# One z unit moved out of the first stage, tile-by-tile pool waits, and block sums between the z units of a DeltaNet encoder layer

## The chip, the cores and the metric

The kernel runs on one NeuronCore of a Trainium2 chip. The core has a matrix engine (TensorE, written PE in the profile, with its weight loads as PEld), a vector engine (VectorE, DVE), a scalar engine (ScalarE, ACT), a small general engine (GpSimd, POOL) and an engine that mostly issues transfers (SyncE, SP). Each engine runs its own instructions in order; they wait for each other through semaphores. SBUF is the on-chip memory, PSUM holds the results of matrix products in eight banks, and transfers between the chip's main memory and SBUF are DMAs. The metric is device time in microseconds; lower is better.

## The reference

The layer works on 1024 tokens plus 16 learned ones, with 1024 features, all in float32. What matters here is the combined input projection and where its columns go:

```python
h = rmsnorm(h_res, norm1_w[l])
proj = h @ w_in[l]
(q, k, v, z, b_raw, a_raw, sc_b, sc_c, sc_x, gate_a, gate_b) = jnp.split(proj, SPLIT_POINTS, axis=-1)
o_dn = gated_deltanet_bidir(q, k, v, z, ...)     # ends with o * silu(z), 8 heads of 128 columns
y_a = o_dn @ w_branch_dn[l]
y_b = (sc_b * conv3(sc_c * sc_x)) @ w_branch_sc[l]
merged = sigmoid(gate_a) * y_a + sigmoid(gate_b) * y_b
h_res = h_res + merged @ w_out[l]
h2 = rmsnorm(h_res, norm2_w[l]); gu = h2 @ w_gate_up[l]
h_res = h_res + (silu(gu[..., :D_FF]) * gu[..., D_FF:]) @ w_down[l]
out = rmsnorm(h_res, final_norm_w)
```

So z is needed for each of 8 heads, and gate_a and gate_b are two 1024-column products that share the moving operand h.

## The kernel before, in words

**Float32 by parts.** Every operand is split into a high part (a rounded copy, made by ACT in `split`, line 101) and a low part (the rest, made by DVE, line 102). A product of 128 features is then three matmuls: high by high, high by low, low by high. A z unit, which is the z of one head for all 1024 tokens, is two halves of 512 tokens; a half is `dense` (lines 134 to 136): 8 blocks of features by 3, so 24 matmuls of 128x128 by 128x512 into one PSUM bank. A unit is 48 such matmuls.

**The first stage** (pools `c1`, `d1`, `dn`; closed by `ph1.close()`) runs the projections of q, k and v, the short convolution, some gates and some z units as PE work, and beside it the scans of the eight heads, each a long chain of small operations on all engines. A planner written into the kernel (the times in `T`, the lanes, `run_streams`, `pump`) decides while the kernel is built how the two are interleaved; the order of all engines is then fixed by `manual_schedule`. Units are taken from `fill_units`, whose last entries are the z units of heads 0 to `ZH`-1 (`u_z`, line 341 for the matmuls, 474 and 478 for the tanh and the product on ACT and DVE, 480 for the transfer to `z_d`). `ZH` is 5. The last steps of the last head are the scaling of its rows (line 936, DVE), their transposes on PE (line 98), the copies to `vS` (951, ACT) and the transfer to `o_d` (953).

**The section behind it.** A new pool, `tp`, takes the SBUF range of the three closed pools. It is opened with the default waits: its first use waits until everything that used the closed pools is over, transfers too. Weights of the z units come through pools that stay open (`wload`, with two buffers `wh`/`wl` in turn; raw data through two raw buffers, and two more of `tp`). The section has the z units of heads 5, 6 and 7 (`z_rows`: line 1502 is the tanh on ACT, 1504 the product on DVE, 1505 the transfer), then the remaining gates.

**The remaining gates** go by pairs: gate_a and gate_b of 128 columns together, five pairs (`GH`=3 pairs were done in the first stage). They use a Strassen scheme of seven half-size products instead of eight. It needs sums of blocks on both sides. On the moving side `moving_sums` makes T1, T2, T3 and T4 from the blocks of h once, in steps of a few large DVE operations (lines 179 and 1409, 128x2048 elements each) and ACT casts (line 1457). On the weight side, each pair splits the raw gate weights (`first`), then `second` splits one block and forms the sums of blocks S1 to S4 (`sums`, lines 1416 and 179) and splits those (`stationary2`). The seven products of a pair (`product`, line 1440, 12 matmuls each) are, in the order of the code: A11·B11, A12·B21, S2·T2, S1·T1, S3·T3, S4·B22, A22·T4. S2·T2, S3·T3 and A22·T4 go on in the bank of A11·B11; S4·B22 goes on in the bank of S1·T1. Between two products in one bank the bank is read: line 1543 copies A11·B11 (ACT), 1555 copies behind S2·T2 (ACT), 1557 copies behind S1·T1 (ACT), and line 1409 adds from a bank on DVE, followed by a tanh (line 1508) on ACT.

**What sets the order.** From the opening of `tp` to the end of pair 0 (`border0`), DVE, PE and ACT issue their instructions of that region in the order of the code (`manual_schedule` for these three engines). Later work, which has no fixed order, may still be put between them: the framework's scheduler, which plans with its own model of times, takes an instruction of later code where it believes an engine to be free and the inputs to be ready. SP is free in this sense too. Behind `border0` all order is the scheduler's.

**PSUM banks** come in three groups: `pm` (2 banks, `psm`), `pe` (3 banks, `psd`), `pd` (3 banks, `pss`). `psz` takes from the first two in turn, `psany` from all three. The z units use `psany`.

## Time and profile before

| | |
|---|---|
| median of 3 runs | 2007.11 us (2007.06 to 2009.29) |
| profiled execution | 2003.46 us, of which its span 2001.7 us |
| mean granted TensorE clock | 0.996 |
| PE busy | 1974.2 us (99%) |
| PE weight loads busy | 1720.7 us (86%) |
| DVE busy | 1398.8 us (70%) |
| ACT busy | 837.2 us (42%) |

Times in the profile count from the first instruction of the span. The matmuls of 512 columns start 0.227 us apart when nothing holds them up, while each is listed with 0.39 us because they are pipelined; so a busy PE is not always at its rate, and gaps are best read from starts. A row of the timeline gives start, duration, engine, line, operation, output and inputs by the program's names, shapes, and the number of merged instructions; what stands in square brackets is the idle time of the engine before it and what ended it. "issue" stands where nothing in the profile ended the wait. In the windows, each row is a stretch of time with the busy time of each engine, the number of its instructions, the granted clock, and the DMA load.

### The profile page before, as it was taken

How to read it: one execution, taken by the hardware profiler on the slowest of the kernel's cores; microseconds unless marked ns; L12 is line 12 of the kernel's file. 1: busy time of each engine (PE TensorE's matmuls, PEld its weight loads, DVE VectorE, ACT ScalarE, POOL GpSimd, SP SyncE). 2: the span in 40 equal slices, each digit the busy share in tenths (PEclk: the TensorE clock that was granted, in tenths of full speed). 3: DMA queues.
4: the chain of work that ended last, by engine and by line, in shares of the span. 5: the costliest groups of instructions: out<-in, count | busy, mean ns of one | idle time of the engine just before them, and what ended most of it. 6: DMA issues, size and time to landing. Idle time of an engine off the chain costs nothing.

```text
span 2001.7 us, 31862 instructions
## 1 busy us (share of the span) xinstructions
PE 1974.2 (99%) x11999; PEld 1720.7 (86%) x11999; DVE 1398.8 (70%) x3020; ACT 837.2 (42%) x1964; POOL 108.0 (5%) x407
## 2 busy tenths in 40 slices
PE   9999999999999999999899999999999999999998
PEld 8999999999999999888688888887888888888887
DVE  6888688888888888844945544469866666656575
ACT  6472354636464646343344221224323333334344
POOL 2011101010101010100000000000000000000000
PEclk9999999999999999999999999999999999999999
DMA  3122221212222212222236743123666345477654
GB/s 133 65 90 74 59 86 59 75 59 75 59 75 59 86 59 65 75 85 91 94 112 239 248 151 112 63 85 107 240 231 216 140 150 188 157 276 244 193 170 172
DMA packets 124689, 251.00 MB, mean 125 GB/s; under 512 B 44981, under 2 KB 46438, under 8 KB 122103
## 3 DMA queue, kind: packets, MB, share of 16 engines
q1 hardware_dynamic: 123959, 247.92, 37.2%
q8 instruction: 94, 1.54, 0.3%
q10 hardware_dynamic: 576, 1.05, 0.1%
q14 instruction: 60, 0.49, 0.1%
HBM read 180.67 MB, written 68.25 MB: 124 GB/s over the span
## 4 chain that ended last, share of the span: by engine, by line
PE 47%; DVE 3%; ACT 1%; issue 1%; DMA 1%; SPq 0%; DVEq 0%; ACTq 0%
PE pd L1440 13%; PE pe L1440 6%; PE pm L1440 4%; PE pe L1894 1%; PE pe L1895 1%; PE pe L1896 1%; PE pd L1894 1%; PE pd L1895 1%; PE pd L1896 1%; PE pd L135 1%; PE pd L134 1%; PE pe L135 1%; PE pe L134 1%; PE pd L136 1%; PE pe L136 1%; PE pm L1895 1%
## 5 line engine op out<-in xcount | busy, mean ns | idle before, releaser
L341 PE MATMUL pm<-hTh,wh 128*128 128x320 f32 (+4 forms) x1264 | 434.2, 349 | 0.4 <-ACT hTh L1103 0.2
L341 PE MATMUL pm<-al,wh 128*128 128x320 f32 (+4 forms) x1264 | 433.6, 348 | 0.0
L341 PE MATMUL pm<-hTh,wl 128*128 128x320 f32 (+4 forms) x1264 | 431.7, 347 | 0.0
L341 PEld LDWEIGHTS pm<-hTh,wh 128*128 128x128 f32 x1264 | 236.7, 188 | 12.6 <-issue 1.3
L341 PEld LDWEIGHTS pm<-hTh,wl 128*128 128x128 f32 x1264 | 237.0, 188 | 10.9 <-issue 0.4
L341 PEld LDWEIGHTS pm<-al,wh 128*128 128x128 f32 x1264 | 236.9, 188 | 10.3
L102 DVE TENSOR_TENSOR al<-raw,ring_h 128x1024 fp32r<-128x1024 f32 x73 | 88.6, 1223 | 64.8 <-ACT ring_h L101 64.4
L101 ACT CAST ring_h<-raw 128x1024 fp32r<-128x1024 f32 x73 | 76.8, 1053 | 107.1 <-PE pe L1896 35.5
L363 DVE SCALAR_TENSOR_TENSOR kq<-ra,wc,kq 128x520 f32<-128x520 f32 x128 | 96.6, 755 | 4.9 <-ACT kq L393 4.0
L990 DVE TENSOR_TENSOR wl<-raw,wh 128x512 fp32r<-128x512 f32 x114 | 77.4, 689 | 31.1 <-ACT wh L993 30.6
L889 ACT ACTIVATE w<-pd,small 128x128 f32<-128x128 f32 x128 | 39.8, 363 | 125.0 <-PE pd L882 124.3
L101 ACT CAST wh<-raw 128x1024 fp32r<-128x1024 f32 x48 | 50.4, 1050 | 77.7 <-PE pd L135 18.7
L500 DVE TENSOR_TENSOR fP<-fP,tm 128x135 f32<-128x135 f32 (+23 forms) x248 | 71.7, 289 | 5.1
L496 DVE TENSOR_TENSOR tm<-fP,fN 128x135 f32<-128x135 f32 (+23 forms) x248 | 71.5, 288 | 4.4
L993 ACT CAST wh<-raw 128x512 fp32r<-128x512 f32 x114 | 67.4, 621 | 3.7 <-issue 3.6
L102 DVE TENSOR_TENSOR wl<-raw,wh 128x1024 fp32r<-128x1024 f32 x48 | 58.5, 1220 | 13.6 <-ACT wh L101 13.4
L1409 DVE TENSOR_TENSOR b<-pd,b 128x512 f32<-128x512 f32 x22 | 15.2, 690 | 66.2 <-PE pd L1440 66.2
L1831 ACT ACTIVATE b<-b 128x512 f32<-128x512 f32 x22 | 13.9, 632 | 113.3 <-DVE b L1409 113.3
L1440 PE MATMUL pd<-b_hl,wh 128*128 128x512 f32 x176 | 54.4, 390 | 0.0
L856 ACT ACTIVATE jk<-NP 128x128 f32<-128x128 f32 x64 | 19.9, 311 | 78.8 <-DVE NP L852 77.7
L1440 PE MATMUL pd<-b,mB 128*128 128x512 f32 x204 | 50.7, 398 | 1.1 <-ACT s L1543 1.1
L876 DVE SCALAR_TENSOR_TENSOR r<-pd,negEG,vS 128x128 f32<-128x128 f32 x120 | 36.7, 345 | 20.9 <-PE pd L866 20.5
(590 smaller groups left out, 4724.6 us busy)
## 6 DMA issues: line engine op xcount, KB each, us to landing
raw<-in_w_in_dram SPq DMA_DIRECT2D x72, 512.0 KB
raw<-in_w_gate_up_dram SPq DMA_DIRECT2D x44, 512.0 KB
sums<-in_w_down_dram SPq DMA_DIRECT2D x22, 512.0 KB
t_d<-sums SPq DMA_DIRECT2D x11, 1024.0 KB
raw<-s_d SPq DMA_DIRECT2D x44, 256.0 KB
raw<-t_d SPq DMA_DIRECT2D x44, 256.0 KB
act_d<-b SPq DMA_DIRECT2D x43, 256.0 KB
raw<-act_d SPq DMA_DIRECT2D x33, 256.0 KB
```

What stands on the lines that cost most here:

```text
L101: nc.scalar.copy(hi, src)
L102: nc.vector.tensor_tensor(out=lo, in0=src, in1=hi.bitcast(F32), op=ALU.subtract)
L134: mm(po[:m, :n], wh[:, k, :m], xhk[:, t0:t0 + n], start=(k == 0), stop=False)
L135: mm(po[:m, :n], wh[:, k, :m], xlk[:, t0:t0 + n], start=False, stop=False)
L341: mm(po[:, :n], ww[:, k], f(k)[:, t0:t0 + n], start=i == 0, stop=i == 3 * KT - 1)
L363: nc.vector.scalar_tensor_tensor(out=acc, in0=raw[:, h0 + t:h0 + t + hn], scalar=wc[:, t, col:col + 1], in1=acc, op0=ALU.mult, op1=ALU.add)
L496: nc.vector.tensor_tensor(out=tv, in0=fP[:, 0:r, j:j + 1].broadcast_to([P, r, n]), in1=fN[:, j:j + 1, j + 1:32].broadcast_to([P, r, n]), o ...
L500: nc.vector.tensor_tensor(out=fP[:, 0:r, j + 1:32], in0=fP[:, 0:r, j + 1:32], in1=tv, op=ALU.subtract)
L990: nc.vector.tensor_tensor(out=u[1][1][:, k], in0=u[2][:, k], in1=u[1][0][:, k].bitcast(F32), op=ALU.subtract)
L993: nc.scalar.copy(u[1][0][:, k], u[2][:, k])
L1440: mm(po, x[:, k], y, start=k + i == 0 and not add_to, stop=k == 3 and i == 2, skip_group_check=add_to)
L1895: mm(bank[t], h_[:, c], l_[:, hi], start=False, stop=False)
```

## The change

`ZH` goes from 5 to 4: the first stage has four z units, the section behind it four (`z0` to `z3`, heads 4 to 7). Their banks come from `psz` in place of `psany`, so `pd` is left to the pairs. The pool `tp` is opened with `reuse_waits="tile"`: each of its tiles waits for what used its own addresses, and not for everything in the closed pools. `second` is cut in two: `block_sums` (split of one block, sums of blocks) and `second` (the splits of those). The order in the section is written anew: the steps of `moving_sums`, the weights of pair 0 and its block sums stand between the halves of the four z units, and no step is left behind the last z unit. `pair` becomes a generator; between the first two products of pair 0 and the rest of it stand the gate split and the block sums of pair 1. Pairs 0 and 1 are both inside `border0`. In a pair that isn't the last, S4·B22 now stands ahead of S3·T3. The last pair is as before.

```diff
-ZH = 5
+ZH = 4
...
-    tp = ctx.enter_context(tc.tile_pool(name="tp", bufs=1))
+    tp = ctx.enter_context(tc.tile_pool(name="tp", bufs=1, reuse_waits="tile"))
...
-            po = psany()
+            po = psz()
             dense(po, z_units[h - ZH], hx, C0 + META + sl.start, 512)
...
         def second():
+            stationary2(n, ru, rg, ru, A_)
+
+        def block_sums():
             split(*u_hl[n % 2], ru[:, 4:8])
             A_["A22"] = u_hl[n % 2]
             sums(rg, ru, rg[:, 0:4], rg[:, 4:8], ru[:, 0:4], ru[:, 4:8])
-            stationary2(n, ru, rg, ru, A_)
-        return A_, first, second
+        return A_, first, block_sums, second
...
+        else:
+            if n > 1:
+                first()
+                block_sums()
+            product(bank, A_["A11"], "B11")
+            nc.scalar.copy(o1[:, left], bank)
+            po = psz()
+            product(po, A_["A12"], "B21")
+            add(o1[:, left], po, o1[:, left])
+            half_turn(o1[:, left])
+            yield
+            if n:
+                second()
+            bank2 = psz()
+            product(bank, A_["S2"], "T2", True)
+            nc.scalar.copy(o1[:, right], bank)
+            product(bank2, A_["S1"], "T1")
+            nc.scalar.copy(o2[:, right], bank2)
+            yield
+            product(bank2, A_["S4"], "B22", True)
+            add(o1[:, right], bank2, o1[:, right])
+            half_turn(o1[:, right])
+            product(bank, A_["S3"], "T3", True)
+            add(o2[:, right], bank, o2[:, right])
+            half_turn(o2[:, right])
+            yield
+            product(bank, A_["A22"], "T4", True)
+            nc.scalar.activation(o2[:, left], bank, AF.Tanh, scale=0.5)
...
-    z0, z1, z2 = (z_rows(h) for h in range(ZH, H))
+    z0, z1, z2, z3 = (z_rows(h) for h in range(ZH, H))
     z_units.append(wload(w_in, unit(OZ + (ZH + 1) * P)))
     next(z0)
     next(sums_of_blocks)
     next(sums_of_blocks)
     next(z0)
-    z_units.append(wload(w_in, unit(OZ + (H - 1) * P)))
+    z_units.append(wload(w_in, unit(OZ + (ZH + 2) * P)))
     next(sums_of_blocks)
     next(z0)
     next(z1)
-    pair0 = pair_weights(0, GH)
     next(z1)
-    pair0[1]()
+    z_units.append(wload(w_in, unit(OZ + (ZH + 3) * P)))
+    next(sums_of_blocks)
     next(z1)
-    pair0[2]()
     next(z2)
+    weights0 = pair_weights(0, GH)
+    next(z2)
+    weights0[1]()
     next(sums_of_blocks)
     next(z2)
+    next(z3)
+    weights0[2]()
+    weights0[3]()
     next(sums_of_blocks)
+    next(z3)
     next(sums_of_blocks)
-    next(z2)
-    next(sums_of_blocks)
-    for n, j in enumerate(range(GH, KT)):
-        o1 = pair(n, j, *(pair_weights(n, j) if n else pair0))
-        if n == 0:
-            border0.close()
+    next(z3)
+    pair0 = pair(0, GH, *weights0)
+    weights1 = pair_weights(1, GH + 1)
+    next(pair0)
+    weights1[1]()
+    weights1[2]()
+    for _ in pair0:
+        pass
+    pair1 = pair(1, GH + 1, *weights1)
+    for _ in pair1:
+        pass
+    border0.close()
+    for n, j in enumerate(range(GH + 2, KT), 2):
+        for _ in pair(n, j, *pair_weights(n, j)):
+            pass
```

More of the change, by code (lines that the diff above doesn't have):

```diff
@@ L1415, in sums @@
         g0, g1, u0, u1 = rg[:, 0:4], rg[:, 4:8], ru[:, 0:4], ru[:, 4:8]
-        nc.vector.tensor_tensor(out=s1, in0=u0, in1=u1, op=ALU.add)
-        sub(s3, g0, u0)
-        sub(s2, s1, g0)
-        sub(s4_, g1, s2)
+        tt = nc.vector.tensor_tensor
+        tt(out=s1, in0=u0, in1=u1, op=ALU.add)
+        tt(out=s3, in0=g0, in1=u0, op=ALU.subtract)
+        tt(out=s2, in0=s1, in1=g0, op=ALU.subtract)
+        tt(out=s4_, in0=g1, in1=s2, op=ALU.subtract)
     def stationary2(j, ru, sa, sb, A_):
@@ L1530, in second, with pair @@
             sums(rg, ru, rg[:, 0:4], rg[:, 4:8], ru[:, 0:4], ru[:, 4:8])
-            stationary2(n, ru, rg, ru, A_)
-        return A_, first, second
-    def pair(n, j, A_, first, second):
+        return A_, first, block_sums, second
+    def pair(n, j, A_, first, block_sums, second):
         last = j == KT - 1
-        o1, o2 = s4(), s4()
+        o1, o2 = outs[n] = s4(), s4()
         bank = pss()
-        if not last:
-            if n:
-                first()
-            product(bank, A_["A11"], "B11")
-            nc.scalar.copy(o1[:, left], bank)
-            po = psz()
-            product(po, A_["A12"], "B21")
-            add(o1[:, left], po, o1[:, left])
-            half_turn(o1[:, left])
         if last:
             first()
-        if n:
+            block_sums()
             second()
-        bank2 = psz()
-        if not last:
-            product(bank, A_["S2"], "T2", True)
-            nc.scalar.copy(o1[:, right], bank)
-            product(bank2, A_["S1"], "T1")
-            nc.scalar.copy(o2[:, right], bank2)
-            product(bank, A_["S3"], "T3", True)
-            add(o2[:, right], bank, o2[:, right])
-            half_turn(o2[:, right])
-            product(bank2, A_["S4"], "B22", True)
-            add(o1[:, right], bank2, o1[:, right])
-            half_turn(o1[:, right])
-            product(bank, A_["A22"], "T4", True)
-            nc.scalar.activation(o2[:, left], bank, AF.Tanh, scale=0.5)
-        else:
+            bank2 = psz()
             product(bank, A_["S2"], "T2")
@@ L1586, in pair @@
             half_turn(o1[:, right])
+        else:
+            if n > 1:
+                first()
+                block_sums()
+            product(bank, A_["A11"], "B11")
[7 more added lines that the diff above has]
+                second()
+            bank2 = psz()
+            product(bank, A_["S2"], "T2", True)
[12 more added lines that the diff above has]
+            nc.scalar.activation(o2[:, left], bank, AF.Tanh, scale=0.5)
         nc.sync.dma_start(ta_d[j], o1)
         nc.sync.dma_start(tb_d[j], o2)
-        return o1
+        yield
+    outs = {}
     sums_of_blocks = moving_sums()
-    z0, z1, z2 = (z_rows(h) for h in range(ZH, H))
+    z0, z1, z2, z3 = (z_rows(h) for h in range(ZH, H))
     z_units.append(wload(w_in, unit(OZ + (ZH + 1) * P)))
@@ L1601, in encoder_layer @@
     next(z1)
-    pair0 = pair_weights(0, GH)
     next(z1)
-    pair0[1]()
+    z_units.append(wload(w_in, unit(OZ + (ZH + 3) * P)))
+    next(sums_of_blocks)
     next(z1)
-    pair0[2]()
     next(z2)
+    weights0 = pair_weights(0, GH)
+    next(z2)
+    weights0[1]()
     next(sums_of_blocks)
     next(z2)
+    next(z3)
+    weights0[2]()
+    weights0[3]()
     next(sums_of_blocks)
+    next(z3)
     next(sums_of_blocks)
-    next(z2)
-    next(sums_of_blocks)
-    for n, j in enumerate(range(GH, KT)):
-        o1 = pair(n, j, *(pair_weights(n, j) if n else pair0))
-        if n == 0:
-            border0.close()
+    next(z3)
[13 more added lines that the diff above has]
+            pass
+    o1 = outs[KT - 1 - GH][0]
     warm2 = keep.tile([P, 1], F32, name="warm2")
```

## The prediction

> **What bounds the kernel now.** I read the page's head first, then stretches of 10 us around the border behind the first stage, then PE's timeline there, then the chain of waits in that window.

> ```profile
> span 2001.7 us, 31862 instructions
> PE 1974.2 (99%) x11999; PEld 1720.7 (86%) x11999; DVE 1398.8 (70%) x3020; ACT 837.2 (42%) x1964; POOL 108.0 (5%) x407
> ```

> PE is the bound: no edit here removes a matmul, so a gain can only be time in which PE stands or runs slowly. In the stretches (PE, PEld, DVE, ACT, POOL busy; clock; DMA) I look for that:

> ```profile
> 970.00:980.00 10.00, 10.00 (x46) 8.26 (x45) 9.32 (x13) 1.70 (x3) 0.00 (x0) 1.00 0.42 160
> 980.00:990.00 10.00, 5.50 (x25) 4.22 (x23) 9.53 (x7) 3.86 (x5) 0.00 (x0) 0.98 0.33 105
> 990.00:1000.00 10.00, 6.07 (x14) 4.10 (x14) 10.00 (x9) 4.40 (x4) 0.00 (x0) 0.67 0.07 27
> 1000.00:1010.00 10.00, 9.56 (x36) 7.80 (x37) 6.01 (x6) 4.57 (x7) 0.00 (x0) 0.84 0.35 115
> ```

> From 980 to 1000 PE is busy for little more than half, DVE for nearly all, and the clock sinks to 0.67. PE's timeline:

> ```profile
> 945.96 0.39 PE L134 MATMUL pm<-hTh,wh 128*128 128x512 f32 x1
> ...
> 967.50 0.39 PE L136 MATMUL pe<-hTh,wl 128*128 128x512 f32 x1
> ...
> 979.90 0.39 PE L1440 MATMUL pd<-hTh,wh 128*128 128x512 f32 x1
> ...
> 985.12 0.39 PE L1440 MATMUL pm<-hTh,wl 128*128 128x512 f32 x1
> 991.38 0.77 PE L1440 MATMUL pd<-hTh,wh 128*128 128x512 f32 x1 [5.88 <-DVE s L1504]
> ...
> 996.21 0.50 PE L1440 MATMUL pd<-hTh,wl 128*128 128x512 f32 x1
> 998.56 0.50 PE L1440 MATMUL pd<-hTh,wh 128*128 128x512 f32 x1 [1.85 <-DVE s L1504]
> 998.90 0.40 PE L1440 MATMUL pd<-al,wh 128*128 128x512 f32 x1
> 1000.43 4.33 PE L1440 MATMUL pd<-b,mB 128*128 128x512 f32 x12 [1.14 <-ACT s L1543]
> 1004.60 2.90 PE L1440 MATMUL pe<-b,mB 128*128 128x512 f32 x12
> ```

> From 945.96 two z units (96 matmuls) take until 967.50 plus one slot: 21.54 over 95 intervals, 0.2267 us each, PE's rate. The third unit's 48 would then end at 978.61; the next product starts at 979.90, so 1.29 are lost. From 979.90 to 1004.60 there are 24+12+2+12 = 50 matmuls, 11.34 at the rate, in 24.70: 13.36 lost. Together **14.65 us lost**, the whole budget of this change. The 14 matmuls at 991.38 to 998.90 are A11·B11 of pairs 1 and 2, which the scheduler put into the gap; S2·T2 of pair 0 starts at 1000.43. The chain that leads there:

> ```profile
> 948.85 4.16 issue
> 953.10 2.29 DVE mA L179
> ...
> 995.55 2.37 DVE mA L1409 x2
> 998.00 1.90 ACT b L1457
> 999.90 0.49 ACT s L1543
> 1000.43 4.33 PE pd L1440 x12
> ```

> So DVE, from the first sum of blocks (953.10) through the T4 sum, then ACT's cast of T4 and, queued behind it, the copy of A11·B11 that S2·T2 needs. And DVE starts 4 us late:

> ```profile
> L480 SPq DMA_DIRECT2D z_d<-rb x5: 319/320/327, 925.0 to 948.9; - x5
>   DVE mA L179: 4.3, 1
> ```

> (tile `rb`, the second row under "who waited for it"): the pool waited for the first stage's last transfer, issued at 948.9 and over about 4.2 later. `mA` itself lies elsewhere.

> **The change, part by part.**

> *The moved unit.* 48 matmuls, 48 x 0.2267 = 10.88 us, leave the first stage, so the section's first z matmul moves from 945.96 to about 935.1. The total stays. What might be uncovered is the last head's end:

> ```profile
> 933.07 0.28 DVE L936 TENSOR_SCALAR NP<-NP,small 128x128 f32<-128x128 f32 x1
> 934.40 0.60 PE L98 MATMUL pd<-ident,NP 128*128 128x128 f32 x4
> ```

> DVE is through with the last head at 933.35, before the unit that goes begins on PE, so I charge 0. The unit's two products on DVE, its splits and its one or two z transfers go with it; SP is nearly idle there.

> *Pool waits.* The first user of `tp` no longer waits for the z transfer. DVE's last work of the first stage then ends at about 936.5 to 937, and T1 can follow at once; with the old waits it would start at 937.1 + 4.2 = 941.3.

> *The new order.* I walk it with DVE at 2.21 us for a 2048-element operation back to back (2.29 alone), 2.28 for the pair of 1024, 1.14 for a weight's low part, 0.60 for 512, and 1.90, 1.00 and 0.55 for ACT's casts of 2048, 1024 and 512, 0.1 for a hand-over. PE does eight halves of 5.44 from 935.1. The weights of the fourth z unit wait for the buffer that the second unit frees, at 935.1 + 21.8 = 956.9: tanh, cast, and DVE has its low part at 958.8. So DVE, which has come through T1, T2 and the low parts by 955.8, waits 3.0; a start up to 3 us later than 936.5 costs nothing. Then 1.14 + T3 6.70 + 0.60 to 967.2; 2.05 for ACT (high T3, tanh); 0.60; 0.95 for the cast of the gate weights, whose buffer the third unit frees; 1.14, T4's first step 2.21, low T3 2.21, 0.60 to 977.0; one split and four sums 3.0; casts and low parts of S 3.4 (one hand-over of 1.1 in it) to 983.5; T4's second step to 985.7. ACT then casts T4 (1.90), does the last z half's tanh (0.55) and the copy (0.55): **S2·T2 starts at 988.9** in place of 1000.43. PE has been through the z units and two products at 984.0, so it stands for **4.9 us**; nothing can fill this, because pair 1 is now fixed behind pair 0, and pair 2's raw weights come into buffers that pair 0 frees at 983. With the old pool waits the walk gives 990.8, so tile waits are worth 1.9 here (between 0 and 2.3).

> *Clock after that gap.* After the 6.0 us gap of before, eleven intervals from 991.38 to 996.21 took 0.439 each, 2.5 lost over twelve; the twelve from 1000.43 took 4.17 for 2.72, 1.45 lost. I take 2.0, the middle; ends 0 and 3.95. [...]

> *Order inside a pair.* S4·B22 right behind S1·T1 must wait for the copy from their bank, A22·T4 right behind S3·T3 for the add:

> ```profile
> 1007.54 0.59 ACT L1557 COPY s<-pe 128x512 f32<-128x512 f32 x1 [1.21 <-PE pe L1440]
> 1010.32 0.69 DVE L1409 TENSOR_TENSOR s<-pd,s 128x512 f32<-128x512 f32 x1 [2.73 <-PE pd L1440]
> 1011.05 0.63 ACT L1508 ACTIVATE s<-s 128x512 f32<-128x512 f32 x1 [2.43 <-DVE s L1409]
> ```

> S1·T1 from 1004.60 leaves its slot at 1007.32 and the copy ends at 1008.13: 0.85. The next product would follow S3·T3 at 1010.06 and the add ends at 1011.01: 1.0. Pair 1's splits of S now stand behind its half turn on ACT: from A12·B21's slot, 0.26 to the add, 0.69, 0.63, cast 1.05, low part 1.22: 3.9. Pairs 0 and 1 have 0.85 + 1.0 each, pair 1 3.9 besides: **7.6 us of new waits** on PE. In pairs 2 and 3 the order is free, and I cost the swap at nothing: S3's own matmuls cover it. How the scheduler covers such a place shows in the last pair, whose S3 stands in the bank of S2:

> ```profile
> 1072.17 1.07 PE L1440 MATMUL pm<-b,mB 128*128 128x512 f32 x4
> 1073.08 3.00 PE L1440 MATMUL pd<-b,mB 128*128 128x512 f32 x12
> 1075.91 1.98 PE L1440 MATMUL pm<-b,mB 128*128 128x512 f32 x8
> ```

> Four matmuls (0.91) of another bank go ahead, and nothing stands. For pairs 0 and 1, pair 2 can give its first 24 matmuls (5.44): freed buffers at 983 plus a load of 3.8,

> ```profile
> 969.31 0.33 SPq L1521 DMA_DIRECT2D raw<-in_w_in_dram  x1
> 973.11 0.62 ACT L101 CAST u_hl<-raw 128x512 fp32r<-128x512 f32 x1 [2.64 <-DMA raw<-in_w_in_dram]
> ```

> plus cast and low part, so by about 991, ahead of the first wait at 994; its S2 and the rest can follow. All 7.6 could be covered, or none; I take 6.1 covered, since the last pair's was whole but the scheduler's times aren't the chip's: **1.5 left**. `psz` for the z units costs nothing: each bank is read at least 6 us before its next use in the walk.

> *Sum.* Lost before 14.65; after 4.9 + 2.0 + 1.5 = 8.4; gain 6.2. On the profiled execution (2003.46) that gives 1997.2; it stood 3.65 under the median of 2007.11 (spread 2.2), on which I forecast **2000.9**.

> **The rivals.** *Uncovered waits (ends slower).* In pairs 0 and 1 PE's queue has nothing from pair 2 where it waits, because the scheduler's model sees no gap or believes pair 2's weights late. Then 7.6 stand in full, and pair 1's 3.9 may drop the clock once more (2.5): 4.9 + 2.0 + 7.6 + 2.5 = 17.0, 2.3 more than before: 2009.5, and 2011.5 if the first drop costs 3.95. It decides once more than about 5 of the 7.6 stay and the clock falls again. For it: pair 1 can't be moved ahead any more, as it was at 991.38; against it: the last pair.

> *The first stage's end lies bare (slower too).* If the scans' last steps move with the planner's books, PE waits at 935 to 945 for up to the removed 10.88: 8.4 + 10.9 = 19.3, so 2011.8; past 6.2 of waiting the gain is gone. Against it: 933.35.

> *Tile waits change nothing.* If the pool waits as a whole all the same, S2 starts at 990.8: 2002.8.

> *DVE no longer late at all.* If the steps between (3.0, 2.05, 0.95, 1.1 of waiting) shrink so that S2 follows A12 at once, only 1.5 is left: 14.65 - 1.5 = 13.1 gained, 1994. Against it: buffers of z weights come free at PE's pace.

> **How the numbers follow.** Forecast 0.42; uncovered waits 0.25; bare end 0.10; pool as before 0.13; DVE in time 0.10. A measurement here can tell about 0.2% (4 us) from no change. The forecast lies beyond that with 0.38 of its 0.42 (its own range: 1997.3, nothing left of 2.0 and 1.5, to 2005), pool as before with 0.05 of 0.13, DVE in time wholly: faster 0.53. Uncovered waits are within it with 0.14, beyond with 0.11; the bare end 0.03 and 0.07: slower 0.18, same 0.29. The range 1995.5 to 2011 leaves out most of "DVE in time" and the worst of the slower two.

> **What would show it.** Right: the section's first z matmul at about 935 with no gap before it; T1's first operation within 2 us of the first stage's last DVE work and no row of "issue" of 4 us ahead of it; PE without a gap through eight halves; one gap of 4 to 6 us ahead of S2·T2, ended by the ACT copy (it stands in `pair`); small pieces of pair 2's A11·B11 between pair 0's and 1's products. Wrong: gaps of about 0.9 and 1.0 in both pairs and 3.9 in pair 1, a second stretch with a clock under 0.9, a wait for the transposes near 935, or T1 starting 4 us after a z transfer.

## The result, and the profile after

The changed kernel takes 2000.73 us (median of 6 runs, 1999.46 to 2003.42); the kernel before took 2008.8 us beside it (median of 6, 2007.06 to 2009.36). The ratio is 0.9965, with a 95% interval of 0.9953 to 0.9977: 7 us faster, between 4.6 and 9.4 (the two medians as they stand are 8.1 apart). The forecast was 2000.9 us.

The head of the page, the stretches around the border (columns as in the prediction) and PE's timeline of the changed kernel; its profiled execution took 2001.06 us:

```profile
span 1999.3 us, 31850 instructions
PE 1973.1 (99%) x11999; PEld 1719.5 (86%) x11999; DVE 1398.9 (70%) x3019; ACT 837.1 (42%) x1963; POOL 106.5 (5%) x407
```

```profile
980.00:990.00 10.00, 5.54 (x25) 4.26 (x23) 7.34 (x9) 4.52 (x5) 0.00 (x0) 1.00 0.33 113
990.00:1000.00 10.00, 8.92 (x32) 6.98 (x33) 8.26 (x10) 4.46 (x7) 0.00 (x0) 0.83 0.13 52
1000.00:1010.00 10.00, 9.16 (x41) 7.27 (x40) 3.27 (x6) 2.38 (x4) 0.00 (x0) 1.00 0.17 68
```

```profile
936.40 0.40 PE L134 MATMUL pe<-hTh,wh 128*128 128x512 f32 x1
...
985.15 0.39 PE L1441 MATMUL pe<-hTh,wl 128*128 128x512 f32 x1
990.41 4.40 PE L1441 MATMUL pd<-b,mB 128*128 128x512 f32 x12 [4.87 <-ACT s L1572]
994.64 2.90 PE L1441 MATMUL pm<-b,mB 128*128 128x512 f32 x12
998.22 0.50 PE L1441 MATMUL pm<-hTh,mB 128*128 128x512 f32 x1 [0.68 <-ACT s L1584]
1001.08 2.88 PE L1441 MATMUL pd<-b,mB 128*128 128x512 f32 x12
1004.80 3.01 PE L1441 MATMUL pd<-b,w 128*128 128x512 f32 x12 [0.84 <-DVE s L1409]
```

Before, three gaps (5.88, 1.85 and 1.14 us) lay ahead of S2·T2, with a clock of 0.67 from 990 to 1000; now there is one gap ahead of it, and the clock is 0.83 for one stretch. S2·T2 starts at 990.41 in place of 1000.43. What ends the gap is still the copy of A11·B11 (now line 1572), at the end of this piece of the chain of waits:

```profile
985.13 2.28 DVE mA L1409 x2
987.49 0.07 ACT b L1458
987.56 1.73 issue
989.29 0.59 ACT s L1503
989.88 0.48 ACT s L1572
990.41 4.40 PE pd L1441 x12
```

"issue" at 987.56 is the rest of ACT's cast of T4 (the row before it), behind which the last z tanh and the copy are queued.

One measure serves all kernels below: **the border's loss**, the distance from the section's first z matmul to one and the same matmul of the last pair (1084.27 in the changed kernel), less 0.2267 us for each matmul between them. It is 14.9 us in the kernel before and 10.3 in the changed one. The changed kernel's 10.3 are 5.0 of gap, 1.5 of clock (S2·T2 to S1·T1 is 4.23 for 2.72), 0.86 and 1.0 from the end of one product to the start of the next ahead of S4·B22 and A22·T4, 0.14 within S4·B22, and 1.7 in small pieces behind 1004.80; the kernel before had 0.24 of these last.

### The profile page after: what moved, and what is told of

The parts are those of the page before. It is cut to its first block, busy times and chain, and to the rows that moved or that the text cites. A ratio compares the mean times of both kernels' runs of the same rounds, so it can differ in the third digit from the quotient of the medians.

```text
span 1999.3 us, 31850 instructions
## 1 busy us (share of the span) xinstructions
PE 1973.1 (99%) x11999; PEld 1719.5 (86%) x11999; DVE 1398.9 (70%) x3019; ACT 837.1 (42%) x1963; POOL 106.5 (5%) x407
## 3 DMA queue, kind: packets, MB, share of 16 engines
q10 hardware_dynamic: 576, 1.05, 0.1%
## 4 chain that ended last, share of the span: by engine, by line
PE 85%; DVE 8%; ACT 3%; DMA 2%; issue 1%; SPq 0%; DVEq 0%; ACTq 0%
PE pm L341 29%; PE pd L1441 12%; PE pe L1441 5%; PE pm L1441 4%; PE pe L1921 1%; PE pe L1920 1%; PE pe L1919 1%; PE pd L882 1%; PE pd L903 1%; PE pd L866 1%; PE pd L869 1%; PE pd L899 1%; PE pe L603 1%; PE pd L1921 1%; PE pd L1920 1%
## 5 line engine op out<-in xcount | busy, mean ns | idle before, releaser
L341 PE MATMUL pm<-hTh,wh 128*128 128x320 f32 (+4 forms) x1248 | 428.1, 348 | 0.4 <-ACT hTh L1103 0.2
L341 PE MATMUL pm<-al,wh 128*128 128x320 f32 (+4 forms) x1248 | 427.4, 348 | 0.0
L341 PE MATMUL pm<-hTh,wl 128*128 128x320 f32 (+4 forms) x1248 | 425.5, 346 | 0.0
L341 PEld LDWEIGHTS pm<-hTh,wl 128*128 128x128 f32 x1248 | 234.0, 188 | 10.2 <-issue 0.4
L101 ACT CAST ring_h<-raw 128x1024 fp32r<-128x1024 f32 x73 | 76.7, 1054 | 106.7 <-PE pd L1921 36.1
L101 ACT CAST wh<-raw 128x1024 fp32r<-128x1024 f32 x49 | 51.4, 1049 | 67.7 <-PE pm L135 17.5
L1409 DVE TENSOR_TENSOR b<-pd,b 128x512 f32<-128x512 f32 x22 | 15.2, 690 | 65.7 <-PE pd L1441 65.7
```

Source lines behind the costliest of these rows:

```text
L101: nc.scalar.copy(hi, src)
L341: mm(po[:, :n], ww[:, k], f(k)[:, t0:t0 + n], start=i == 0, stop=i == 3 * KT - 1)
```

## The experiments

**The kernel before once more.** No edit; it shows how far two executions differ.

> The kernel before, unchanged, for a second profile. Its first profile was 3 to 5 us under its median, and every comparison of times so far shows about 2.4 us more gain than the traces do. Theory A: the first profile caught a short form of the clock loss behind the 6 us gap (2.5 + 1.45 us); the second shows S2·T2 of pair 0 or the product behind it later or slower by 2 to 4 us, all else within 1 us. Rival: the difference is spread over the span (single short stalls at other places, as the two of 0.6 and 1.5 us that the changed kernel's profile has at 394 and 1495 us).

Ratio 0.9998 (0.9989 to 1.0007), 2005.5 us. The profiled execution has a span of 2004.3 us where the first had 2001.7, and its border's loss is 16.4 where the first had 14.9. Two places carry the difference. One stretch of the border, and one product far behind it:

```profile
1000.00:1010.00 10.00, 9.75 (x32) 7.92 (x33) 5.82 (x6) 4.38 (x7) 0.00 (x0) 0.73 0.25 79
```

```profile
1498.54 3.06 PE L1440 MATMUL pd<-b,w 128*128 128x512 f32 x12 [1.49 <-DVE b L1409]
```

The clock is 0.73 where it was 0.84, and PE waits 1.49 us for a DVE sum; the changed kernel has the same wait (1.45 at 1494.14), the first execution of the kernel before has not. (DVE waits there for a weight transfer, 4.9 us here and 3.6 in the first execution; that this is the cause was not tried.) So each theory has about half of it. The execution that the prediction was summed on was shorter than this one by 2.6 us of span, and a gain read as one trace less another carries a difference of that size.

**Tile waits alone**, on the kernel before.

```diff
-    tp = ctx.enter_context(tc.tile_pool(name="tp", bufs=1))
+    tp = ctx.enter_context(tc.tile_pool(name="tp", bufs=1, reuse_waits="tile"))
```

> The kernel before with the tile-by-tile waits of the pool alone. Theory A (the chain of DVE operations from T1 to the cast of T4 ends in the copy that S2·T2 of pair 0 waits for, and tile waits only let it start earlier): T1 starts right behind the first stage's last DVE product at about 949 instead of 953, S2·T2 up to 4 us earlier, so 2 to 4 us less than before (about 2005 where before is 2008.8). Theory B (the tile waits are the whole gain, the unit that moved does nothing): 7 to 8 us less, about 2001. Theory C (tile waits change nothing): no difference.

2002.05 us beside 2006.5: 0.9979 (0.9971 to 0.9988). S2·T2 starts 3.4 us earlier than before (1000.43):

```profile
997.06 5.49 PE L1440 MATMUL pd<-b,mB 128*128 128x512 f32 x12 [1.15 <-ACT s L1543]
```

T1 starts at 948.49, directly behind the first stage's last product, where it started at 953.10. The border's loss is 13.1. So theory A held, at the upper end of its 2 to 4 us: alone the tile waits are worth 4.2 us of time (2.4 to 5.8), of which 1.8 to 3.3 stand in the border.

**The changed kernel with the old pool waits.**

```diff
-    tp = ctx.enter_context(tc.tile_pool(name="tp", bufs=1, reuse_waits="tile"))
+    tp = ctx.enter_context(tc.tile_pool(name="tp", bufs=1))
```

> The changed kernel with the old pool waits. Theory A: T1 starts at about 943.5 (z transfer issued at 939.3 plus 4.2) instead of 939.2; of these 4.3 us the 1 to 3 us that DVE waits later on in the changed kernel swallow part, so S2·T2 starts 2 to 3 us later and the time is 2 to 3 us above the changed kernel (about 2003). Theory B: the gain is gone, about 2008. Theory C: no difference at all, 2000.7.

2004.21 us, ratio 0.9989 (0.998 to 0.9997) where the changed kernel has 0.9965. DVE's timeline of this kernel first, then of the changed one, and PE's of this one:

```profile
938.07 0.68 DVE L478 SCALAR_TENSOR_TENSOR rb<-rb,pm 128x512 f32<-128x512 f32 x1
943.07 2.29 DVE L179 TENSOR_TENSOR mA<-hTh 128x2048 f32<-128x2048 f32 x1 [4.32 <-DMA z_d<-rb]
```

```profile
938.62 0.68 DVE L478 SCALAR_TENSOR_TENSOR rb<-rb,pm 128x512 f32<-128x512 f32 x1
939.22 2.28 DVE L179 TENSOR_TENSOR mA<-hTh 128x2048 f32<-128x2048 f32 x1
...
959.95 1.23 DVE L102 TENSOR_TENSOR wl<-raw,wh 128x1024 fp32r<-128x1024 f32 x1 [1.16 <-ACT wh L101]
```

```profile
992.95 5.15 PE L1441 MATMUL pd<-b,mB 128*128 128x512 f32 x12 [6.63 <-ACT s L1572]
```

Counted from each kernel's first z matmul (935.84 here, 936.40 there), T1 is 4.4 us later and S2·T2 3.1 later. The 1.16 us in which DVE waits for the fourth unit's weights (959.95) take up most of the difference of 1.3. With slower matmuls behind the longer gap, the border's loss is 14.1, so 3.8 us more.

**S3·T3 ahead of S4·B22 again**, in all pairs but the last.

```diff
             yield
-            product(bank2, A_["S4"], "B22", True)
-            add(o1[:, right], bank2, o1[:, right])
-            half_turn(o1[:, right])
             product(bank, A_["S3"], "T3", True)
...
             half_turn(o2[:, right])
+            product(bank2, A_["S4"], "B22", True)
+            add(o1[:, right], bank2, o1[:, right])
+            half_turn(o1[:, right])
             yield
```

> The changed kernel with S3·T3 ahead of S4·B22 again in the pairs that aren't the last. Theory A (a product that goes on in the bank of the one ahead of it must wait for that bank's reader): the 0.7 and 0.8 us ahead of S4·B22 and A22·T4 in pair 0 go, pair 1 stays covered, 1.5 us less, about 1999.2; this is under what three rounds would tell, so the trace decides. Rival: other waits take their place (the copy behind S1·T1 stands behind three casts on ACT), no change in the two sums.

1996.62 us, ratio 0.9951 (0.9938 to 0.9963). PE's timeline of this kernel:

```profile
989.48 4.61 PE L1441 MATMUL pd<-b,mB 128*128 128x512 f32 x12 [4.87 <-ACT s L1572]
993.93 2.90 PE L1441 MATMUL pm<-b,mB 128*128 128x512 f32 x12
996.67 2.88 PE L1441 MATMUL pd<-b,mB 128*128 128x512 f32 x12
...
1002.11 2.88 PE L1441 MATMUL pd<-b,w 128*128 128x512 f32 x12
```

No wait is left behind S2·T2: S3·T3 runs while S1·T1's bank is copied, S4·B22 while S3·T3's is added. The border's loss is 7.5, so 2.8 less: 1.8 ahead of 1004.80, and 1.0 in pairs 1 to 3, where the loss behind 1004.80 falls from 1.7 to 0.7. There, in the changed order, the scheduler puts pieces of other products into the waits, but a rest of each wait stays. So with A22·T4 of pair 2 in the changed kernel, in PE's timeline and in DVE's:

```profile
1044.53 0.39 PE L1441 MATMUL pd<-hTh,wh 128*128 128x512 f32 x1
1044.85 3.01 PE L1441 MATMUL pd<-b,w 128*128 128x512 f32 x12
```

```profile
1044.10 0.69 DVE L1409 TENSOR_TENSOR s<-pd,s 128x512 f32<-128x512 f32 x1 [1.18 <-DMA raw<-p_d]
```

A22·T4 starts 0.32 behind the matmul ahead of it instead of 0.23, just behind the end of the add (1044.79), and its twelve take 2.85 for 2.72. Counted between these products, S4·B22 first costs about 0.3 in each of pairs 1, 2 and 3.

**The copy early**: pair 0's A11·B11, its copy and A12·B21 ahead of the T4 sum and cast, and S2·T2 and S1·T1 ahead of T4's low part and of pair 1's sums of blocks.

```diff
     weights0[3]()
-    next(sums_of_blocks)
     next(z3)
-    next(sums_of_blocks)
     next(z3)
...
     next(pair0)
+    next(sums_of_blocks)
+    next(pair0)
+    next(sums_of_blocks)
     weights1[1]()
```

> The changed kernel with pair 0's first two products, their copy and their add ahead of T4's sum and cast, and S2·T2 and S1·T1 ahead of T4's low part and pair 1's block sums. Theory A (the 5.0 us gap ahead of S2·T2 is only the copy of A11·B11 that stands on ACT behind the cast of T4, and the slow 4.2 us of S2·T2 is the clock that this gap costs): S2·T2 follows A12·B21 within 0.5 us, the clock stays at 1.00, 5.0 + 1.5 = 6.5 us less, about 1994.5. Rival (DVE's chain as a whole is late, so the gap only moves): PE waits 3 to 5 us ahead of S4·B22 or A22·T4 instead, gain under 2 us.

1996.56 us, ratio 0.9952 (0.9938 to 0.9965). PE's timeline:

```profile
984.47 2.88 PE L1441 MATMUL pd<-b,mB 128*128 128x512 f32 x12
987.19 2.88 PE L1441 MATMUL pm<-b,mB 128*128 128x512 f32 x12
...
991.30 0.50 PE L1441 MATMUL pm<-hTh,mB 128*128 128x512 f32 x1 [1.23 <-ACT s L1584]
...
999.51 3.03 PE L1441 MATMUL pd<-b,w 128*128 128x512 f32 x12 [2.48 <-DVE s L1409]
```

The gap of 5.0 us and the slow matmuls behind it are gone, which shows that the copy, late only because it stood behind the T4 cast on ACT, set the start of S2·T2. But the border's loss falls by 4.4, not by 6.5: the two waits behind it grow, to 1.23 and 2.48.

**Both orders together.** The two edits above in one kernel.

> Copy early and S3·T3 ahead of S4·B22 together. Theory A (both waits are of the kind 'a product waits for the reader of its own bank'): S2·T2 at once behind A12·B21, and the 1.2 and 2.5 us that still stood ahead of S4·B22 and A22·T4 go, since another bank's product lies between; 3 to 4 us under each of the two alone, 12 to 14 us under before. Rival: T4's low part is late on DVE, so 2 us or more stand ahead of A22·T4 all the same, and it is within 1.5 us of the two alone.

1995.38 us, ratio 0.9947 (0.9933 to 0.996); border's loss 5.9, as with the early copy alone: theory A failed. DVE's timeline, then PE's:

```profile
994.23 0.68 DVE L1417 TENSOR_TENSOR raw<-raw 128x512 f32<-128x512 f32 x1
...
997.01 0.68 DVE L1409 TENSOR_TENSOR s<-pd,s 128x512 f32<-128x512 f32 x1
```

```profile
997.75 4.62 PE L1441 MATMUL pd<-b,w 128*128 128x512 f32 x12 [2.36 <-DVE s L1409]
```

The add from S3·T3's bank, for which A22·T4 waits, is queued on DVE behind the four sums of blocks of pair 1 (from 994.23). The rival had the size right and the cause wrong: T4's low part was through at 991.44. The clock falls behind this wait too (0.93 from 990 to 1000, 0.90 from 1000 to 1010): 4.62 us for twelve matmuls.

**Pair 1's sums behind pair 0's adds**, on top of both.

```diff
     weights1[1]()
+    next(pair0)
     weights1[2]()
```

> The order with both edits (S3·T3 first, and the early copy), and with pair 1's four sums of blocks (0.69 us each on DVE) a step later, behind the adds of S3·T3 and S4·B22, which they stood ahead of. Theory A (the 2.36 us ahead of A22·T4 in that order came from these sums standing ahead of the two adds on DVE, and the half clock after it cost 1.9: 12 matmuls took 4.62 us in place of 2.72): A22·T4 starts within 0.7 us of S4·B22's end and at full clock, and the border gains 3.5 to 4.3 us on that order, some 5 to 7 us on the changed kernel; about 1991.5 us where the kernel before takes 2006. Theory B (DVE has the same amount of work ahead of pair 1's S2·T2, whose weights wait for the sums, so the wait only moves): A22·T4 is in time, but a wait of 2 us or more stands ahead of pair 1's S2·T2, and the time stays at 1995 to 1997.

1992.3 us beside 2005.51: ratio 0.9929 (0.9915 to 0.9943), the fastest of all. PE's timeline, DVE's, and the stretches:

```profile
992.09 3.04 PE L1441 MATMUL pd<-b,mB 128*128 128x512 f32 x12 [0.74 <-ACT s L1582]
...
997.69 2.88 PE L1441 MATMUL pd<-b,w 128*128 128x512 f32 x12
```

```profile
995.17 0.69 DVE L1409 TENSOR_TENSOR s<-pd,s 128x512 f32<-128x512 f32 x1
...
1000.51 0.69 DVE L1417 TENSOR_TENSOR raw<-raw 128x512 f32<-128x512 f32 x1
```

```profile
990.00:1000.00 10.00, 9.26 (x41) 7.31 (x41) 6.16 (x6) 6.21 (x8) 0.00 (x0) 1.00 0.08 31
1000.00:1010.00 10.00, 10.00 (x45) 7.95 (x43) 8.93 (x14) 5.51 (x8) 0.00 (x0) 1.00 0.43 158
```

Theory A held: the border's loss is 1.6, 4.3 less than with both orders; the wait did not move to pair 1, for whose weights there was time.

**The gap filled with work that nothing uses**, in the changed kernel.

```diff
             bank2 = psz()
+            if n == 0:
+                for k in (0, 1, 2, 3, 0, 1):
+                    for x, y, i in ((0, 0, 0), (0, 1, 1), (1, 0, 2)):
+                        m = mov["B21"][y]
+                        mm(bank2, A_["A12"][x][:, k], m[k] if isinstance(m, list) else m[:, k], ...)
             product(bank, A_["S2"], "T2", True)
```

> The changed kernel with 18 matmuls more, of A12·B21 once more into the bank that S1·T1 overwrites afterwards, between A12·B21 and pair 0's S2·T2: work that nothing uses, 4.1 us of the 4.9 us gap. Theory A (the gap lowers the clock, and S2·T2's 12 matmuls take 4.23 us in place of 2.72 for that alone): S2·T2 starts where it did, 990.4 give or take 0.3, its 12 take 2.7 to 2.9 us, and the border ends 1.2 to 1.6 us earlier; ratio to the kernel before about 0.9958 where the changed kernel had 0.9965. Theory B (the waits behind it are for DVE and ACT, so that matmuls at full clock only wait longer ahead of S4·B22 and A22·T4): the 12 take 2.7 us, but the two waits of 0.68 and 0.84 us grow by what is saved, and the ratio stays at 0.9965.

```profile
988.12 3.06 PE L1441 MATMUL pd<-b,mB 128*128 128x512 f32 x12 [0.80 <-ACT s L1572]
991.01 2.88 PE L1441 MATMUL pm<-b,mB 128*128 128x512 f32 x12
994.71 0.50 PE L1441 MATMUL pm<-hTh,mB 128*128 128x512 f32 x1 [0.82 <-ACT s L1589]
...
1001.29 3.01 PE L1441 MATMUL pd<-b,w 128*128 128x512 f32 x12 [0.84 <-DVE s L1409]
```

Counted from the first z matmul (934.10 here), S2·T2 starts at 54.02 us, in the changed kernel at 54.01; its twelve take 2.89 from start to start in place of 4.23, and the granted clock is 1.00 in all stretches from 980 to 1030. The idle time alone had made them slow, and 1.34 is its price here. The wait ahead of S4·B22 grows from 0.68 to 0.82, the other stays; the border ends 1.2 us earlier. The time does not show it: 1998.69 us beside 2005.51, ratio 0.9965 (0.9952 to 0.9978), the changed kernel's own ratio. So theory A is shown in the trace and not in the time.

**The unit back in the first stage**, with the new order and the tile waits kept. In short:

```diff
-ZH = 4
+ZH = 5
...
-    z0, z1, z2, z3 = (z_rows(h) for h in range(ZH, H))
+    z0, z1, z2 = (z_rows(h) for h in range(ZH, H))
```

with the steps of the sums and of pair 0's weights put between the halves of three units.

> The changed kernel with five z units in the first stage and three behind it again; tile waits, order of the pairs and steps as changed. Theory A (the fourth unit covers 10.9 us of the DVE chain): z section from about 946, T1 at about 949, S2·T2 at 991 to 994 with PE through the two products at 984 to 985, so a gap of 7 to 9 us and a longer slow clock: 3 to 6 us above the changed kernel (about 2003 to 2006 where it is 2000). Rival (order and tile waits are the gain): same time as the changed kernel.

2006.97 us beside 2005.98: 1.0001 (0.9992 to 1.001). PE's timeline, and one stretch:

```profile
996.01 5.49 PE L1441 MATMUL pd<-b,mB 128*128 128x512 f32 x12 [11.29 <-ACT s L1572]
```

```profile
990.00:1000.00 10.00, 3.99 (x9) 3.14 (x10) 7.09 (x7) 4.33 (x5) 0.00 (x0) 0.50 0.45 156
```

T1 starts at 948.84 on DVE here, since the first stage's last z product stands ahead of it, and PE has one unit less to do meanwhile. The gap is 11.29 us, above the 7 to 9 expected, the border's loss 18.6. Without the moved unit the new order and the tile waits gain nothing; in this order the unit makes the difference from 1.0001 to 0.9965, some 7 us. But tile waits alone, in the old order, gave 0.9979. So the new order without the unit costs what the tile waits gain; its gap has none of the 14 matmuls of pairs 1 and 2 that stood in the gap before, which may be why. Order and unit together add 0.0014, some 3 us, to the tile waits; the two intervals overlap, and the border's loss falls by 2.8 (13.1 to 10.3). What the unit is worth in the old order was not tried.

**One unit more**, five behind the first stage.

```diff
-ZH = 4
+ZH = 3
...
-    z0, z1, z2, z3 = (z_rows(h) for h in range(ZH, H))
+    z0, z1, z2, z3, z4 = (z_rows(h) for h in range(ZH, H))
```

> One more unit moved: three z units in the first stage, five behind it. The gap of 5.0 us ahead of S2·T2 and its slow clock are covered in full (5 to 6.5 us less). Theory A (the z units are the only PE work beside the last head's scan steps, which end at about 934): PE waits inside the first stage between 915 and 935 for up to the 10.9 us that went, and the kernel is 2 to 5 us slower than the changed one. Rival: the scheduler puts the section's first z unit among the scan steps, nothing is bare, and it is 5 to 6 us faster than the changed one.

1999.77 us, ratio 0.9966 (0.9952 to 0.9979): the same time as with four. PE's timeline at the end of the first stage and at S2·T2:

```profile
931.19 0.53 PE L98 MATMUL pd<-ident,NP 128*128 128x128 f32 x2 [0.35 <-DVE NP L936]
...
989.30 4.41 PE L1441 MATMUL pd<-b,mB 128*128 128x512 f32 x12 [2.71 <-ACT s L1572]
```

The end of the scans isn't bare: the scheduler puts z matmuls of the section among their last steps (the first at 923.39), and the wait there is 0.35 us. So neither theory held. T1 starts 6.8 us earlier (932.42 for 939.22), but S2·T2 only 1.1, and a gap of 2.71 is left. The time between is spent in the chain, which now waits for PE: in this order the cast of pair 0's block (ACT, 976.24) stands behind the tanh of a z half that keeps PE until 975.5, and DVE waits 3.19 us for the cast. An order with the block sums earlier was not tried.

## Why the prediction was right

The time came as forecast (2000.73 for 2000.9). The main step, a fourth unit and tile waits that leave one gap of 5 us ahead of S2·T2, was right; that the number fits to 0.2 us is luck, since steps that were partly off offset each other.

- **Moved unit, nothing charged.** Right. No gap stands ahead of 936.40 and none in the eight halves. The start is 1.3 us later than 935.1, of which 0.7 arise at 389 and 394 us, within the first stage. The rival of the bare end falls twice, even with five units behind.
- **Tile waits.** The mechanism was right, T1 directly behind line 478. The size was not: 1.9 (0 to 2.3) was forecast, and the old waits cost 3.1 of S2·T2's start and 3.8 in all. The mis-sized term is the 3.0 us that DVE was to wait for the fourth unit's weights; it waits 1.16. The rival that the tile waits change nothing falls with both runs on it.
- **The walk to S2·T2, and the gap.** From the first z matmul 53.8 us were forecast and 54.0 measured; 4.9 of gap, and 5.0. Right, the slack of DVE apart.
- **Clock after the gap.** 2.0 forecast; 1.5 measured, and 1.34 of it shown by filling the gap. The granted clock is 0.50 from 989.98 to 993.40 and 1.00 on both sides, which makes the 0.83 from 990 to 1000. The smaller of the two losses of before, 1.45, came nearer than their middle. That the second slow stretch of before would not come back was right too.
- **Order inside a pair.** 7.6 of new waits, 6.1 covered, 1.5 left: measured 1.9 left in pair 0 and 0.7 in pair 1. Pair 1's 3.9 was covered as forecast but for 0.4, by matmuls of pair 2 (1013.09 on), and its two short ones but for 0.3. Pair 0's two were not: the low part of pair 2's first weights came not by 991, but here, in DVE's timeline of the changed kernel:

```profile
996.28 1.22 DVE L102 TENSOR_TENSOR wl<-raw,wh 128x1024 fp32r<-128x1024 f32 x1
```

  That ends at 997.50, behind the start of the first wait (997.36). The second wait, from 1003.80, it would have reached; the scheduler put none of pair 2 there, why was not tried.
- **The swap in pairs 2 and 3, costed at nothing.** This failed, though it is small. The order S4·B22 first costs 1.0 behind 1004.80, in the rests of waits that the scheduler's pieces leave, about 0.3 in each of pairs 1 to 3. With the 1.8 in pair 0, which the prediction did count, that is 2.8 by the run that undoes it.
- **Sum.** In the terms of the prediction 9.3 are lost up to pair 1's A22·T4 where 8.4 were forecast; with the pairs behind it, put at nothing, 10.3. Against the first execution of the kernel before (14.9) that is 4.6 us less in the border, not 6.2; against the second (16.4) it is 6.1, and the 7 us of the times lie between 4.6 and 9.4. The wait of 1.49 us far behind does not add to this, since the changed kernel has it too. The prediction added its 3.65 us between profile and median without knowing from where. Counted from the 2008.8 us that the kernel before took beside the changed one, the same gain of 6.2 would have given 2002.6.
- **Uncovered waits.** This rival had the place right in pair 0 and failed for the most part in pair 1: 2.6 of the 7.6 stood, under the 5 from which it decides, and the clock did not fall a second time (1.00 from 993.40 to 1385.93).
- **DVE in time.** Not so here, but near: with the copy ahead of T4's cast S2·T2 follows A12·B21 at once. The rival sought the change in DVE's waiting; it lay in ACT's queue.

## What to carry to other kernels

When an instruction that frees a bank is queued behind a long one that it doesn't need, put it ahead; then look at once for the next queue that does the same, since the first two such edits gained 2.8 and 4.4 us but together only 4.4 us of the border's loss, and the third (one line, four sums moved behind two adds) took off 4.3 more. Filling a bound engine's gap from a stage where it had the same work anyway is worth it only as long as the chain on the other engines does not in turn wait for that work: in the new order the first moved unit was worth some 7 us, the next one nothing. An order made for a moved unit can cost without it what another part of the change gains, so a change of three parts is best taken apart from both ends, each part alone and each part left out. Before two traces are subtracted, a second execution of the same kernel shows how much of the difference is the execution's own, here 2.6 us of span.

## What was not expected of the hardware

```profile
995.25:998.66 3.41, 1.05 (x5) 0.77 (x5) 2.97 (x5) 0.93 (x2) 0.00 (x0) 1.00 0.00 0
998.66:1002.07 3.41, 3.41 (x10) 2.63 (x9) 0.00 (x0) 0.29 (x1) 0.00 (x0) 0.50 0.38 154
```

```profile
994.63:998.04 3.41, 2.41 (x11) 1.67 (x9) 3.31 (x5) 0.00 (x0) 0.00 (x0) 1.00 0.00 0
998.04:1001.45 3.41, 1.94 (x8) 1.61 (x9) 1.42 (x3) 1.23 (x2) 0.00 (x0) 1.00 0.33 132
```

  The first wait lies in one piece, PE stands for 2.36 of its 3.41 us, and the next piece has half the clock. The second is cut in two, 1.00 and 1.47, and the clock stays. Over the twelve traces (30 to 1985 us), each of the 24 pieces at full clock in which PE stood for 1.9 us or more was followed by half the clock (in the kernel before and the changed one these are five, with 2.48 to 3.41 us); where it stood for 1.8 or less this came once (1.30 us, near 290 in the kernel with the unit back).
- The slow clock is 0.50 from 989.98 to 993.40 in the changed kernel, 3.4 us. Lost share times 2 times 10 us, summed over the stretches from 980 to 1010, is one, two, three or four times that, or nothing: 3.4 us in the changed kernel (0.83), 6.8 with the old pool waits (0.66), 10.2 with the tile waits alone (0.96, 0.67, 0.86), 13.6 in the second execution of the kernel before (0.92, 0.67, 0.73), 0 with the early copy (1.00 in all three).
- Going from one bank to another cost nothing by itself: in the changed kernel A11·B11 of pair 1 ends in `pd` with the matmul at 1010.14 and A12·B21 begins in `pe` at 1010.37, 0.23 later. Starts that came later stand right behind what they need: S2·T2 of pair 1 at 1016.56 behind the end of ACT's cast of its weights at 1016.52, A22·T4 of pair 2 at 1044.85 behind its add.
